# Reading the moving operand of the float32r matmuls as two interleaved streams

## The chip, the cores and the metric

The kernel runs on one core of a Trainium2 chip. The time is the device time of one execution in microseconds (us), the median of three runs. The engines are named as in the profile: PE is TensorE (matmuls), PEld its weight loads, DVE is VectorE, ACT is ScalarE, POOL is GpSimd, and SP is the engine that issues most of the DMA transfers.

## What is computed

One decoder layer on a sequence of 1024 tokens with 1024 channels, all float32: a pooling mixer with a residual, then a gated FFN with a short causal convolution and a second residual.

```python
def reference(x, ...):                      # x (1, 1024, 1024)
    h = rms_norm(x, norm_mix_g[0])
    x = x + pool_mixer(h, pool_w[0], pool_b[0], pool_scale[0])
    f = conv_ffn(rms_norm(x, norm_ffn_g[0]), ffn_w_in[0], ffn_conv_w[0], ffn_conv_b[0], ffn_w_out[0])
    return x + f

def conv_ffn(x, w_in, conv_w, conv_b, w_out):
    h = causal_depthwise_conv(x @ w_in, conv_w, conv_b)   # w_in (1024, 5632), conv over 3 tokens
    val, gate = jnp.split(h, 2, axis=-1)
    return (jax.nn.silu(gate) * val) @ w_out              # w_out (2816, 1024)
```

Nearly all the work is in the two matrix products of the FFN, x @ w_in and the last one.

## The kernel before

**Mixer.** For each of 8 blocks of 128 tokens, plain float32 matmuls form the window sums (psd, L191) and the pooled projection (psy, L274). The residual goes to x1_dram (L281), and the normed block n2 is turned by PE (`ffn_operand`, L303): eight transposes against an identity matrix (pst, L307) give a bank of 128 channels by 128 tokens for each of eight groups of channels. From there ACT and DVE write the operands of the first product.

**First product.** Both products are done with a seven-product block scheme (steps P1 to P7) in place of eight. Its operands are sums and differences of quarters of the two matrices. The token side of the first product stands in tiles B11, B21, T1, T2, T3, B22 and T4 (each 128 partitions, 4 groups of channels, 512 tokens). Each number is stored as two float32r parts, the rounded value and the rest (`split_n`, L323), and each product of two numbers is made from three of the four part products. `product` (L381) runs 12 matmuls into one bank: weights as stationary operand (128x128), 512 tokens as moving operand. There are 22 x 7 such calls, 1848 matmuls. Banks X, Y and Z are read by ACT and DVE (`step`), go through the convolution along the tokens (`conv`), the gate, and are stored in g_dram (L446).

**Second product.** Blocks of g_dram (stationary) and w_out (moving, 512 output channels) are loaded, summed and split by `prep_out` and `split` (L77). The loop over `oevents` runs 4 x 3 matmuls for each event (L744) into four banks, 924 in all, each bank taking eleven events of a step or of two. `z_add` (L660) adds the banks to the residual tiles z by DVE, and the last addition of each tile is followed by its store to `out`. The last bank is done in two halves, the second of them in a bank of its own named rest (L732), so that the first half's add and store run beside the second half's matmuls.

**Order.** The order on each engine is that of the recorded program. Steps P1 to P7 follow a fixed list (`events`), operands are prepared five events ahead (LOOK), in the second product two (OLOOK), with at most about four DVE operations for each event. Columns of all moving operands are read in the order in which they lie.

Of the kernel before, what the change touches and what calls it, by code (L numbers as in the profile page):

```python
# [7 lines left out]
F32 = mybir.dt.float32  # L8
F32R = mybir.dt.float32r
BF16 = mybir.dt.bfloat16  # L10
AF = mybir.ActivationFunctionType
ALU = mybir.AluOpType
PSUM = bass.MemoryType.PSUM

P = 128
# [3 lines left out]
NS = S // P  # L19
NK = D // P  # L20
# [25 lines left out]
NH = 512  # L46
HALVES = [slice(0, NH), slice(NH, D)]
NP2 = NF // 2


@with_exitstack
def trunk_kernel(ctx: ExitStack, tc: tile.TileContext, x, consts, par, rows, pool_w, w_in, w_out, out):
    nc = tc.nc
# [69 lines left out]
    for g, w in enumerate(WINDOWS):  # L123

        m = band[:, g, :]
# [26 lines left out]
    fac = cst[:, FAC:E0].rearrange("p (c t) -> p c t", t=HALO)  # L152
    band_e = cst[:, E0:ID].bitcast(BF16).rearrange("p (g s) -> p g s", s=P)
    ident = cst[:, ID:]
# [79 lines left out]
    def gain_rows():  # L234
        ps = bank2("ps_gain")
        for k in range(NK):
            gain = par_sb[:, GF + k : GF + k + 1].to_broadcast([P, P])
            marks["gain_pe"] = nc.tensor.matmul(ps[:, k * P : (k + 1) * P], gain, ident, start=True, stop=True).ins
        gain_b = pp.tile([P, D], F32, tag="gain_b", name="gain_b")
        marks["gain"] = nc.scalar.activation(gain_b, ps, AF.Copy, scale=FOLD).ins  # L240
        return gain_b
# [61 lines left out]
    def ffn_operand(j):  # L303
        n2 = n2s.pop(j)
        ps = bank2(f"pst{j}")
        for c in range(NK):
            nc.tensor.transpose(ps[:, c * P : (c + 1) * P], n2[:, c * P : (c + 1) * P], ident)  # L307
        cols = slice(j * P, (j + 1) * P)
        ps3 = ps.rearrange("p (c s) -> p c s", c=NK)
        lo, hi = slice(0, 4), slice(4, 8)  # L310
        if j < NS // 2:
            split_n(nops["B11"], ps3[:, lo, :], cols)
            split_n(nops["B21"], ps3[:, hi, :], cols)
            nc.scalar.activation(n2f[:, :, cols], ps3, AF.Copy)
            return
        cols0 = slice(cols.start - NH, cols.stop - NH)
        b11, b12, b21, b22 = n2f[:, lo, cols0], ps3[:, lo, :], n2f[:, hi, cols0], n2f[:, hi, cols]
        nc.scalar.activation(b22, ps3[:, hi, :], AF.Copy)
        sub(b11, b11, b12)
        split_n(nops["T1"], b11, cols0)  # L320
        sub(n2f[:, lo, cols], b22, b12)

    def split_n(t, src, cols=slice(None), ks=slice(None)):  # L323
        h = t[:, 0, ks, cols]
        nc.scalar.activation(h, src, AF.Copy)
        nc.vector.tensor_tensor(t[:, 1, ks, cols], src, h.bitcast(F32), ALU.subtract)  # L326


    order = [j + k * NP2 for j in range(NP2) for k in range(2)]
# [6 lines left out]
    def sub(out, a, b):  # L336
        nc.vector.tensor_tensor(out, a, b, ALU.subtract)  # L337

    def add(out, a, b):
        nc.vector.tensor_tensor(out, a, b, ALU.add)  # L340
# [40 lines left out]
    def product(bank, a, b, opens):  # L381
        m = 0
        for k in range(4):
            ks = slice(k * P, (k + 1) * P)
            for i, l in ((0, 0), (0, 1), (1, 0)):
                nc.tensor.matmul(bank, a[:, i, ks], b[:, l, k, :], start=opens and m == 0, stop=m == 11, skip_group_check=not opens)  # L386
                m += 1

    STEPS = {
# [270 lines left out]
    def z_add(name, set_, rows_, cols, last, rest=None):  # L660
        banks_ = [obanks[set_, i] for i in range(4)]

        def go(i):
            parts = [(slice(0, NH), banks_[i])]
            if rest is not None and i == 3:
                parts = [(slice(0, NH // 2), banks_[i][:, : NH // 2]), (slice(NH // 2, NH), rest[:, : NH // 2])]
            for c, bank in parts:
                z = zs[name, i][:, c]
                add(z, bank, z)
                if last:  # L670
                    r = rows_ * NH + i * P
                    nc.sync.dma_start(out[r : r + P, s_half[cols]][:, c], z)

        chores.extend((go, (i,)) for i in range(4))

# [13 lines left out]
    for k in range(-SLOOK, len(oevents)):  # L689
        p, f = oevents[k + SLOOK] if k + SLOOK < len(oevents) else (None, 0)  # L690
        for _ in range({"P1": 2, "P2": 1, "P5": 1}.get(p, 0)):
            asked[todo[0]] = k + SLOOK
            load_block(*todo.pop(0))
        for name in {"P2": ("A12", "B21"), "P3": ("A12",), "P4": ("B21",)}.get(p, ()):
            load_stream(name, f)
        if k < -OLOOK:
            continue

        with tc.issue_after(lasts[-1]) if lasts else nullcontext():
            room = 4  # L700
            if k + OLOOK < len(oevents):
                e = oevents[k + OLOOK]
                for name in NEEDS.get(e[0], ()):
                    if (name, e[1]) in ahead:
                        do_sum(name, e[1])
                        ahead.remove((name, e[1]))
                        room -= 1
                oops[e] = prep_out(*e)
                room -= 2 + (e[0] in ("P3", "P4"))
            if k < 0:  # L710
                continue
            p, f = oevents[k]
            if chores and f:
                do, args = chores.pop(0)
                for i in args:
                    do(i)
                room -= 1
            while room > 0 and ahead and k >= earliest(*ahead[0]):
                do_sum(*ahead.pop(0))
                room -= 1  # L720
        set_, opens = chains[p]
        if f == 0 and opens:
            for i in range(4):
                tag = ("XXYY" if set_ == "X" else "YZZZ")[i]
                pool = ps_x if tag == "X" else ps_yz
                obanks[set_, i] = pool.tile([P, NH], F32, tag=tag, name=f"o{p}{i}")

        if k >= len(oevents) - TAIL:
            if f < NP2 - 1:
                continue  # L730

            rest = ps_yz.tile([P, NH], F32, tag="Z", name="rest")  # L732
            second = slice(NH // 2, NH)
            add(zs["z21", 3][:, second], obanks[set_, 3][:, second], zs["z21", 3][:, second])
            steps = [(i, g, slice(0, NH), obanks[set_, i]) for i in range(3) for g in range(NP2 - TAIL, NP2)]
            steps += [(3, g, c, t[:, : NH // 2]) for c, t in ((slice(0, NH // 2), obanks[set_, 3]), (second, rest)) for g in range(NP2 - TAIL, NP2)]
        else:
            steps = [(i, f, slice(0, NH), obanks[set_, i]) for i in range(4)]
        for i, g, c, bank in steps:
            a, b = oops[p, g]  # L740
            alone = opens and (p, i) != ("P4", 3)
            for m, (u, v) in enumerate(((0, 0), (0, 1), (1, 0))):
                first = g == (NP2 - TAIL if c.start else 0) and m == 0
                nc.tensor.matmul(  # L744
                    bank, a[:, u, i * P : (i + 1) * P], b[:, v, c],
                    start=opens and first, stop=g == NP2 - 1 and m == 2, skip_group_check=not alone,
                )
        if f == NP2 - 1:
            if p == "P1":
                for i in range(4):  # L750
                    zs["q1", i] = z_tile("q1", i)
                    nc.scalar.activation(zs["q1", i], obanks["X", i], AF.Copy)
                z_start("z11", 0, 0)
            elif p == "P2":
                z_add("z11", "Y", 0, 0, True)
                z_start("z22", 1, 1)
            elif p == "P5":
                z_add("z22", "X", 1, 1, False)
                z_start("z12", 0, 1)
            elif p == "P6":  # L760
                z_add("z12", "Y", 0, 1, False)
            elif p == "P3":
                z_add("z12", "X", 0, 1, True)
                z_start("z21", 1, 0)
            elif p == "P7":
                z_add("z22", "Y", 1, 1, True)
                z_add("z21", "Y", 1, 0, False)
            else:
                z_add("z21", "X", 1, 0, True, rest)
                while chores:  # L770
                    do, args = chores.pop(0)
                    for i in args:
                        do(i)


def constants():
# [11 lines left out]
    def packed(blocks):  # L788
        bits = np.concatenate(blocks, axis=1).astype(np.float32).view(np.uint32)
        assert not (bits & 0xFFFF).any()  # L790
        return np.ascontiguousarray((bits >> 16).astype(np.uint16)).view(np.float32)

    blocks = [packed(first)] + fac + [packed(edge), np.eye(P)]
    return np.concatenate([b.astype(np.float32) for b in blocks], axis=1)


# [32 lines left out]
```

## Time and profile before

| | |
|---|---|
| median of 3 runs | 700.12 us (699.56 to 700.15) |
| the profiled execution | 699.62 us, span 697.7 us |
| HBM traffic | 85.49 MB by DMA, mean 123 GB/s |
| granted TensorE clock | 1.0 in the whole span |

The page gives the busy time of each engine, the busy share in 40 slices of the span, and groups of instructions:

```profile
PE   9999999999999999999999999999999999999998
DVE  4798999999888888888898888876887988999985
DMA  8873113222221211222222221329989700122131
L79 ACT ACTIVATE oBP<-blk 128x512 fp32r<-128x512 f32 x53 | 33.5, 633 | 49.0 <-PE oP L744 32.2
L80 DVE TENSOR_TENSOR oBP<-blk,oBP 128x512 fp32r<-128x512 f32 x53 | 36.6, 691 | 13.3 <-ACT oBP L79 13.3
```

A digit is the busy share of a slice of 17.4 us in tenths, 9 for 90% or more. A group row reads: line, engine, operation, tile written and tiles read, partitions by elements, count; then busy time in us, mean ns of one; then the idle time of the engine just before them and what ended most of it. The length of a matmul in a row holds the time in which it overlaps the next, so the distance from one to the next is shorter than the row's mean. The mixer ends at about 75 us, the first product at 485 us, the second at 694.5 us.

### The profile page before, as it was taken

What the parts mean: (1) busy time and instruction counts of PE and PEld (TensorE: products, weight loads), DVE (VectorE), ACT (ScalarE), POOL (GpSimd) and SP (SyncE); (2) the same over time, 40 slices, a digit from 0 to 9 for tenths busy, and PEclk for the clock granted to TensorE, in tenths of its full rate; (3) what the DMA queues carried; (4) which work ended last, traced back from release to release, by engine and by line L of the source; (5) the groups of instructions that cost most, each with busy time, mean ns of one, the idle gap of its engine ahead of it and who ended that gap; (6) DMA issues with size and microseconds to landing.
All of it is one profiled execution on the core that took longest, in us unless ns stands there. A gap on an engine that the chain in (4) does not pass through costs nothing.

```text
span 697.7 us, 8537 instructions
## 1 busy us (share of the span) xinstructions
PE 692.2 (99%) x3164; PEld 575.5 (82%) x3164; DVE 596.4 (85%) x881; ACT 344.0 (49%) x517; POOL 13.2 (2%) x33
## 2 busy tenths in 40 slices
PE   9999999999999999999999999999999999999998
PEld 7898778888888888888888888888888888888886
DVE  4798999999888888888898888876887988999985
ACT  6787645544444445444454444445454344444431
POOL 3020000000000000000000000000000000000000
PEclk9999999999999999999999999999999999999999
DMA  8873113222221211222222221329989700122131
GB/s 275 296 189 116 62 60 111 102 90 92 91 82 70 88 48 76 92 92 90 91 90 92 89 80 73 99 91 348 326 298 341 273 20 0 61 90 90 63 106 62
DMA packets 32706, 85.49 MB, mean 123 GB/s; under 512 B 3708, under 2 KB 5400, under 8 KB 29848
## 3 DMA queue, kind: packets, MB, share of 16 engines
q1 hardware_dynamic: 31472, 82.83, 33.8%
q0 software_dynamic: 1184, 2.11, 1.8%
q8 instruction: 25, 0.41, 0.2%
q14 instruction: 17, 0.14, 0.1%
q10 hardware_dynamic: 8, 0.00, 0.0%
HBM read 62.89 MB, written 19.92 MB: 119 GB/s over the span
## 4 chain that ended last, share of the span: by engine, by line
PE 92%; DVE 4%; DMA 1%; ACT 1%; issue 1%; SPq 0%; DVEq 0%; ACTq 0%
PE oP L744 30%; PE Y L386 24%; PE Z L386 16%; PE X L386 16%; PE psy L274 3%; PE psd L191 1%; DVE T L326 1%; DMA x<-in_x_dram 1%; PE pst L307 1%; PE psy L277 0%; DVE n2f L337 0%; DVE n2f L562 0%; DVE n2f L555 0%; ACT junk_a L168 0%; PE ps_edges L191 0%
## 5 line engine op out<-in xcount | busy, mean ns | idle before, releaser
L744 PE MATMUL oP<-oBP,oAP 128*128 128x512 f32 (+1 forms) x924 | 208.8, 388 | 0.0
L744 PEld LDWEIGHTS oP<-oBP,oAP 128*128 128x128 f32 x924 | 172.9, 188 | 36.0 <-DVE oBP L80 0.3
L386 PE MATMUL Z<-T,S1s 128*128 128x512 f32 x264 | 64.1, 390 | 0.3 <-DVE T L326 0.2
L386 PE MATMUL X<-B,A11s 128*128 128x512 f32 x264 | 64.2, 390 | 0.0
L386 PE MATMUL Y<-T,S2s 128*128 128x512 f32 x264 | 63.7, 389 | 0.2 <-ACT S2s L79 0.2
L386 PE MATMUL X<-B,A12s 128*128 128x512 f32 x264 | 63.5, 389 | 0.0
L386 PE MATMUL Y<-T,A22s 128*128 128x512 f32 x264 | 63.4, 389 | 0.0
L386 PE MATMUL Y<-T,S3s 128*128 128x512 f32 x264 | 63.4, 389 | 0.0
L386 PE MATMUL Z<-B,S4s 128*128 128x512 f32 x264 | 63.3, 389 | 0.0
L386 PEld LDWEIGHTS Z<-T,S1s 128*128 128x128 f32 x264 | 49.4, 188 | 11.5 <-DVE T L326 0.7
L386 PEld LDWEIGHTS Y<-T,S2s 128*128 128x128 f32 x264 | 49.5, 188 | 10.8 <-ACT S2s L79 0.6
L386 PEld LDWEIGHTS Y<-T,A22s 128*128 128x128 f32 x264 | 49.5, 188 | 10.4
L386 PEld LDWEIGHTS Z<-B,S4s 128*128 128x128 f32 x264 | 49.6, 188 | 10.3
L386 PEld LDWEIGHTS Y<-T,S3s 128*128 128x128 f32 x264 | 49.5, 188 | 10.3
L386 PEld LDWEIGHTS X<-B,A11s 128*128 128x128 f32 x264 | 49.3, 188 | 10.5 <-DVE A11s L80 0.4
L386 PEld LDWEIGHTS X<-B,A12s 128*128 128x128 f32 x264 | 49.5, 188 | 10.2
L79 ACT ACTIVATE oBP<-blk 128x512 fp32r<-128x512 f32 x53 | 33.5, 633 | 49.0 <-PE oP L744 32.2
L80 DVE TENSOR_TENSOR oBP<-blk,oBP 128x512 fp32r<-128x512 f32 x53 | 36.6, 691 | 13.3 <-ACT oBP L79 13.3
L444 ACT ACTIVATE gate<-gate 128x1024 f32<-128x1024 f32 x22 | 23.3, 1061 | 41.9 <-DVE gate L435 41.9
L79 ACT ACTIVATE oAP<-blk 128x512 fp32r<-128x512 f32 x55 | 34.1, 621 | 19.2 <-DVE blk L337 15.9
L340 DVE TENSOR_TENSOR win<-win 128x512 f32<-128x512 f32 x60 | 41.1, 687 | 1.1
L80 DVE TENSOR_TENSOR oAP<-blk,oAP 128x512 fp32r<-128x512 f32 x55 | 37.7, 685 | 2.6 <-ACT oAP L79 2.6
(132 smaller groups left out, 937.8 us busy)
## 6 DMA issues: line engine op xcount, KB each, us to landing
win<-in_w_in_dram SPq DMA_DIRECT2D x22, 1024.0 KB, 4.8
g_dram<-val SPq DMA_DIRECT2D x22, 512.0 KB, 2.6
blk<-g_dram SPq DMA_DIRECT2D x33, 256.0 KB, 5.2
blk<-in_w_out_dram SPq DMA_DIRECT2D x31, 256.0 KB, 5.9
A12s<-g_dram SPq DMA_DIRECT2D x22, 256.0 KB, 5.1
B21s<-in_w_out_dram SPq DMA_DIRECT2D x22, 256.0 KB, 2.8
x_dram<-x SPq DMA_DIRECT2D x8, 512.0 KB, 2.7
z<-x_dram SPq DMA_DIRECT2D x16, 256.0 KB, 5.3
```

The lines of the kernel that those rows point to most:

```text
L79: nc.scalar.activation(t[:, 0, :], src, AF.Copy)
L80: m = nc.vector.tensor_tensor(t[:, 1, :], src, t[:, 0, :].bitcast(F32), ALU.subtract)
L191: m = nc.tensor.matmul(ps[:, c * P : (c + 1) * P], src[:, c * P : (c + 1) * P], weights[:, c // 2, :], start=True, stop=True)
L274: nc.tensor.matmul(o, dh[:, c, :], wps[:, c, :], start=c % 4 == 0, stop=False, skip_group_check=True)
L307: nc.tensor.transpose(ps[:, c * P : (c + 1) * P], n2[:, c * P : (c + 1) * P], ident)
L326: nc.vector.tensor_tensor(t[:, 1, ks, cols], src, h.bitcast(F32), ALU.subtract)
L340: nc.vector.tensor_tensor(out, a, b, ALU.add)
L386: nc.tensor.matmul(bank, a[:, i, ks], b[:, l, k, :], start=opens and m == 0, stop=m == 11, skip_group_check=not opens)
L444: nc.scalar.activation(gate, gate, AF.Silu)
L744: nc.tensor.matmul(bank, a[:, u, i * P : (i + 1) * P], b[:, v, c], start=opens and first, stop=g == NP2 - 1 and m == 2, skip_group_check=n ...
```

## The change

The 512 columns of the moving operand are read in the order 0, 256, 1, 257 and so on to 255, 511: two streams of 256 in turns (`woven`). To leave the results as they were, the columns are stored or read elsewhere in the order that goes with it.

- First product: the tokens in the operand tiles are stored with even tokens in the first 256 places and odd ones in the second. The identity matrix that turns the tokens has its columns in the order even, odd (`turn`), so a turned block of 128 tokens comes as 64 even and 64 odd ones, and ACT and DVE write two runs of 64 in place of one of 128. Read in turns, the columns come in the order of the tokens, so the banks and what follows are unchanged.
- Second product: w_out lies as before. Read in turns, its channels 0, 256, 1, 257 and so on come to the bank in that order, and who reads the bank (`z_add` on DVE, the copy q1 on ACT) takes the places 0, 2, 4 ... for channels 0 to 255 and 1, 3, 5 ... for the rest (`apart`). The halves of the last bank are now the channels 0 to 127 with 256 to 383, and the rest.

```diff
+def woven(t):
+    return t.rearrange("p (a b) -> p b a", a=2)
+def apart(bank):
+    return bank.rearrange("p (b a) -> p a b", a=2)
+def halved(t, n=2):
+    return t.rearrange("p (a b) -> p a b", a=n)
...
-            marks["gain_pe"] = nc.tensor.matmul(ps[:, k * P : (k + 1) * P], gain, ident, start=True, stop=True).ins
+            marks["gain_pe"] = nc.tensor.matmul(ps[:, k * P : (k + 1) * P], gain, woven(ident), start=True, stop=True).ins
...
-        ps3 = ps.rearrange("p (c s) -> p c s", c=NK)
+        ps3 = ps.rearrange("p (c a s) -> p c a s", c=NK, a=2)
...
+        half, q = divmod(j, NS // 2)
+        cols = slice(q * P // 2, (q + 1) * P // 2)
+        here, first = (n2f[:, :, h * NH : (h + 1) * NH].rearrange("p c (a s) -> p c a s", a=2)[:, :, :, cols] for h in (half, 0))
...
-                nc.tensor.matmul(bank, a[:, i, ks], b[:, l, k, :], start=opens and m == 0, stop=m == 11, skip_group_check=not opens)
+                nc.tensor.matmul(bank, a[:, i, ks], woven(b[:, l, k, :]), start=opens and m == 0, stop=m == 11, skip_group_check=not opens)
...
-                z = zs[name, i][:, c]
-                add(z, bank, z)
+                z = halved(zs[name, i])[:, :, c]
+                add(z, apart(bank), z)
...
-                    bank, a[:, u, i * P : (i + 1) * P], b[:, v, c],
+                    bank, a[:, u, i * P : (i + 1) * P], woven(b[:, v, :])[:, c.start // 2 : c.stop // 2, :],
...
-                    nc.scalar.activation(zs["q1", i], obanks["X", i], AF.Copy)
+                    nc.scalar.activation(halved(zs["q1", i]), apart(obanks["X", i]), AF.Copy)
...
-    blocks = [packed(first)] + fac + [packed(edge), np.eye(P)]
+    turn = np.eye(P).reshape(P, P // 2, 2).transpose(0, 2, 1).reshape(P, P)
+    blocks = [packed(first)] + fac + [packed(edge), turn]
```

No instruction is added, removed or moved on any engine; PE's and POOL's rows differ in their line numbers alone. What differs on the others is the shape of some accesses. ACT, where it takes turned tokens from the banks pst into the tiles B and n2f, before:

```order
L325 ACTIVATE B_155<-pst_411 128x4x128
L168 ACTIVATE junk_b_401,st_b_402<-x_146 128x1024
L325 ACTIVATE B_157<-pst_411 128x4x128
L169 ACTIVATE st_b_402<-st_b_402,eps_t 128x1
L168 ACTIVATE junk_a_431,st_a_432<-x_231 128x1024
L314 ACTIVATE n2f<-pst_411 128x8x128
```

and the same place now:

```order
L338 ACTIVATE B_155<-pst_411 128x8x64
L180 ACTIVATE junk_b_401,st_b_402<-x_146 128x1024
L338 ACTIVATE B_157<-pst_411 128x8x64
L181 ACTIVATE st_b_402<-st_b_402,eps_t 128x1
L180 ACTIVATE junk_a_431,st_a_432<-x_231 128x1024
L328 ACTIVATE n2f<-pst_411 128x8x2x64
```

The order stands, and each group of 128 tokens is written as two runs of 64. DVE at the end of the program, with the last additions to the output tiles z, before:

```order
L80 TENSOR_TENSOR oBP_10_5498<-B21s_5452,oBP_10_5498 128x512
L340 TENSOR_TENSOR z_0_5184<-oP_5322,z_0_5184 128x512
L340 TENSOR_TENSOR z_1_5186<-oP_5323,z_1_5186 128x512
L340 TENSOR_TENSOR z_2_5207<-oP_5324,z_2_5207 128x512
L340 TENSOR_TENSOR z_3_5209<-oP_5325,z_3_5209 128x256
L340 TENSOR_TENSOR z_3_5209<-rest,z_3_5209 128x256
```

and now:

```order
L92 TENSOR_TENSOR oBP_10_5498<-B21s_5452,oBP_10_5498 128x512
L353 TENSOR_TENSOR z_0_5184<-oP_5322,z_0_5184 128x512
L353 TENSOR_TENSOR z_1_5186<-oP_5323,z_1_5186 128x512
L353 TENSOR_TENSOR z_2_5207<-oP_5324,z_2_5207 128x512
L353 TENSOR_TENSOR z_3_5209<-oP_5325,z_3_5209 128x2x128
L353 TENSOR_TENSOR z_3_5209<-rest,z_3_5209 128x2x128
```

The additions are as many and as large; the halves of the last tile are two runs of 128 channels each.

More of the change, by code (lines that the diff above doesn't have):

```diff
@@ L307, in ffn_operand, with split_n @@
             nc.tensor.transpose(ps[:, c * P : (c + 1) * P], n2[:, c * P : (c + 1) * P], ident)
-        cols = slice(j * P, (j + 1) * P)
-        ps3 = ps.rearrange("p (c s) -> p c s", c=NK)
+        ps3 = ps.rearrange("p (c a s) -> p c a s", c=NK, a=2)
         lo, hi = slice(0, 4), slice(4, 8)
[L311 to L314, printed above, removed]
+        half, q = divmod(j, NS // 2)
+        cols = slice(q * P // 2, (q + 1) * P // 2)
+        here, first = (n2f[:, :, h * NH : (h + 1) * NH].rearrange("p c (a s) -> p c a s", a=2)[:, :, :, cols] for h in (half, 0))
+        if half == 0:
+            split_n(nops["B11"], ps3[:, lo], cols)
+            split_n(nops["B21"], ps3[:, hi], cols)
+            nc.scalar.activation(here, ps3, AF.Copy)
             return
-        cols0 = slice(cols.start - NH, cols.stop - NH)
-        b11, b12, b21, b22 = n2f[:, lo, cols0], ps3[:, lo, :], n2f[:, hi, cols0], n2f[:, hi, cols]
-        nc.scalar.activation(b22, ps3[:, hi, :], AF.Copy)
+        b11, b12, b22 = first[:, lo], ps3[:, lo], here[:, hi]
+        nc.scalar.activation(b22, ps3[:, hi], AF.Copy)
         sub(b11, b11, b12)
[L320 to L324, printed above, removed]
+        split_n(nops["T1"], b11, cols)
+        sub(here[:, lo], b22, b12)
+    def split_n(t, src, cols=None, ks=slice(None)):
+        h, l = (t[:, i, ks] if cols is None else t[:, i].rearrange("p k (a s) -> p k a s", a=2)[:, :, :, cols] for i in range(2))
         nc.scalar.activation(h, src, AF.Copy)
-        nc.vector.tensor_tensor(t[:, 1, ks, cols], src, h.bitcast(F32), ALU.subtract)
+        nc.vector.tensor_tensor(l, src, h.bitcast(F32), ALU.subtract)
     order = [j + k * NP2 for j in range(NP2) for k in range(2)]
@@ L663, in go @@
         def go(i):
-            parts = [(slice(0, NH), banks_[i])]
+            parts = [(slice(0, NH // 2), banks_[i])]
             if rest is not None and i == 3:
-                parts = [(slice(0, NH // 2), banks_[i][:, : NH // 2]), (slice(NH // 2, NH), rest[:, : NH // 2])]
+                parts = [(slice(0, NH // 4), banks_[i][:, : NH // 2]), (slice(NH // 4, NH // 2), rest[:, : NH // 2])]
             for c, bank in parts:
-                z = zs[name, i][:, c]
-                add(z, bank, z)
+                z = halved(zs[name, i])[:, :, c]
+                add(z, apart(bank), z)
                 if last:
                     r = rows_ * NH + i * P
-                    nc.sync.dma_start(out[r : r + P, s_half[cols]][:, c], z)
+                    nc.sync.dma_start(halved(out[r : r + P, s_half[cols]])[:, :, c], z)
         chores.extend((go, (i,)) for i in range(4))
@@ L733, in trunk_kernel @@
             second = slice(NH // 2, NH)
-            add(zs["z21", 3][:, second], obanks[set_, 3][:, second], zs["z21", 3][:, second])
+            z = halved(zs["z21", 3])[:, :, NH // 4 :]
+            add(z, apart(obanks[set_, 3][:, second]), z)
             steps = [(i, g, slice(0, NH), obanks[set_, i]) for i in range(3) for g in range(NP2 - TAIL, NP2)]
```

## The prediction

> **What bounds the kernel now.** I read the page from the top: the busy times, then the chain of work that ended last, then the groups on that chain. The profiled execution took 699.62 us for a span of 697.7 us; the median of the three timed runs is 700.12 us, 0.07% more, so a sum made against 699.6 us stands for the median too.
>
> ```profile
> span 697.7 us, 8537 instructions
> PE 692.2 (99%) x3164; PEld 575.5 (82%) x3164; DVE 596.4 (85%) x881; ACT 344.0 (49%) x517; POOL 13.2 (2%) x33
> PE oP L744 30%; PE Y L386 24%; PE Z L386 16%; PE X L386 16%; PE psy L274 3%; PE psd L191 1%; DVE T L326 1%; DMA x<-in_x_dram 1%; PE pst L307 1%; PE psy L277 0%; DVE n2f L337 0%; DVE n2f L562 0%; DVE n2f L555 0%; ACT junk_a L168 0%; PE ps_edges L191 0%
> L744 PE MATMUL oP<-oBP,oAP 128*128 128x512 f32 (+1 forms) x924 | 208.8, 388 | 0.0
> L386 PE MATMUL Z<-T,S1s 128*128 128x512 f32 x264 | 64.1, 390 | 0.3 <-DVE T L326 0.2
> ```
>
> TensorE (PE) is busy 99% of the span, and the two lines that the change touches, L386 and L744, hold 86% of the chain. Seven groups like the last row (7 x 264 = 1848) and the 924 of L744 make 2772 matmuls. They wait for nothing (0.3 us and 0.0 us of idle time). So the time is 2772 times the distance from one matmul to the next, plus the stage before. That distance is not the 388 ns of a row, since matmuls overlap; the chain in order of time gives it, with start, length and count:
>
> ```profile
> 484.75 208.67 PE oP L744 x924
> 346.04 2.72 PE Z L386 x12
> 46.09 3.46 PE psy L274 x16
> 50.01 0.87 PE pst L307 x8
> 44.30 1.79 PE psd L191 x16
> ```
>
> In both products a matmul of 512 columns takes 2.72/12 = 226.7 ns (208.67/924 = 225.8 ns, with some short ones in it). [...] The plain float32 matmuls ahead of them are slower per column: psy, 256 columns, 3.46/16 = 216.3 ns; pst, 128 columns, 0.87/8 = 108.8 ns; psd, 128 columns, 1.79/16 = 111.9 ns. The merged timeline shows the shorter form of the float32r matmul, and the groups of PE and of weight loads by shape give the rest:
>
> ```profile
> 693.26 1.24 PE L744 MATMUL rest<-oBP,oAP 128*128 128x256 f32 x9
> L744 PE MATMUL rest<-oBP,oAP 128*128 128x256 f32 x9 | 1.2, 283 | 0.0
> L386 PEld LDWEIGHTS Y<-T,S2s 128*128 128x128 f32 x264 | 49.5, 188 | 10.8 <-ACT S2s L79 0.6
> L274 PEld LDWEIGHTS psy<-wps,dh 128*128 128x128 f32 x128 | 23.9, 190 | 3.1
> ```
>
> A float32r matmul of 256 columns takes (1.24 - 0.283)/8 = 119.6 ns. From 512 to 256 columns the difference is 107.1 ns, 0.418 ns a column, which leaves 2 x 119.6 - 226.7 = 12.5 ns per matmul that do not depend on the columns. The same for plain float32, 256 against 128 columns: 0.84 ns a column and 2 x 108.8 - 216.3 = 1.3 ns fixed with pst, 0.815 ns a column and 2 x 111.9 - 216.3 = 7.5 ns with psd. The weight load is the same (188 and 190 ns, 128x128). So **a matmul whose columns arrive every 0.42 ns pays 5 to 11 ns of fixed cost that one with columns every 0.84 ns does not pay.**
>
> **The change, part by part.** No instruction is added, removed or moved on any engine; only the patterns differ.
>
> (1) The moving operand of all 2772 matmuls. Column 0 is followed by column 256, then 1, 257, and so on: two places 1 KB apart, each advancing one column per 0.84 ns, which is the pace of the plain float32 products. No row of this trace shows such a read. Its cost is bounded by the rows above: at best the fixed 12.5 ns go; at worst a column costs 0.84 ns instead of 0.418 ns. The row nearest in pace for each stream is that of the plain products, with 1.3 to 7.5 ns fixed. I take 2.5 ns, nearer to pst, because a pst is one instruction per call, as a float32r matmul is. That is 10 ns less per matmul, with -12.5 and +203 to +212 ns as the far ends.
>
> What of the 10 ns is on the path is read by stages, with DVE (VectorE) beside PE:
>
> ```profile
> core 0: us, PE busy (x) PEld busy (x) DVE busy (x) ACT busy (x) POOL busy (x), PEclk, DMA share, GB/s
> 64.00:102.00 38.00, 37.46 (x174) 29.91 (x173) 37.81 (x52) 21.79 (x32) 0.00 (x0) 1.00 0.20 70
> 102.00:160.00 58.00, 58.00 (x257) 48.04 (x256) 56.31 (x75) 30.84 (x43) 0.00 (x0) 1.00 0.26 91
> 160.00:484.00 324.00, 324.00 (x1431) 268.38 (x1430) 272.80 (x351) 152.69 (x205) 0.00 (x0) 1.00 0.27 95
> 484.75:693.42 208.67, 208.67 (x927) 172.79 (x926) 181.77 (x286) 92.29 (x154) 0.00 (x0) 1.00 0.43 149
> ```
>
> Up to 102 us DVE is busy 37.81 of 38.00 us: nothing is gained there, since PE would only wait for DVE. From 102 to 160 us, 257 x 10 ns = 2.6 us would be saved, but DVE has 56.31 us to do in 58.00 us, so 1.7 us at most: what is late next is DVE, which preps the next operands. From 160 to 484 us: 324/0.2267 = 1429 matmuls x 10 ns = 14.3 us; DVE at 272.80 us fits into 309.7 us. Second product: 924 x 10 ns = 9.2 us; DVE's 181.77 us fits into 199.5 us. DMA moves 149 GB/s there at a share of 0.43. Together -25.2 us.
>
> [...]
>
> (2) Reads of banks with step 2: each output bank is now read as even and odd places.
>
> ```profile
> L340 DVE TENSOR_TENSOR z<-oP,z 128x512 f32<-128x512 f32 x27 | 18.4, 683 | 3.3 <-PE oP L744 3.3
> L340 DVE TENSOR_TENSOR z<-z,q 128x512 f32<-128x512 f32 x16 | 10.9, 683 | 0.0
> L752 ACT ACTIVATE q<-oP 128x512 f32<-128x512 f32 x4 | 2.2, 592 | 0.1
> L340 DVE TENSOR_TENSOR z<-rest,z 128x256 f32<-128x256 f32 x1 | 0.4, 425 | 0.7 <-PE rest L744 0.7
> ```
>
> The last of these rows is in the tail, see (4). Some 28 adds of 683 ns (27 and halves) read a bank. An add from a bank costs what one from SBUF costs (683 ns both), so the place of the operand does not set the pace, and step 2 is likely free: I take 0, with +683 ns each, 19 us of DVE, as the other end (below nothing is excluded, as the same elements are read). Cover: DVE has 208.67 - 181.77 = 26.9 us free in the second product, 17.7 us if PE is faster. At the dear end DVE would have 200.9 us to do against 199.5 us, and the stage would keep 1 us less of its gain, or up to 9 us where several adds fall together. The four q copies (592 ns, ACT busy 92 of 209 us) are hidden at either end.
>
> (3) Tokens written in runs of 64 instead of 128 (L325, L318, L314, L337 on ACT and DVE).
>
> ```profile
> L325 ACT ACTIVATE B<-pst 128x512 fp32r<-128x512 f32 x8 | 4.7, 592 | 2.1 <-PE pst L307 2.0
> L326 DVE TENSOR_TENSOR B<-pst,B 128x512 fp32r<-128x512 f32 x8 | 5.5, 688 | 0.5 <-ACT B L325 0.3
> L258 DVE TENSOR_TENSOR psd<-psd,edges 128x128 f32<-128x128 f32 x6 | 1.8, 294 | 1.7 <-ACT edges L203 1.1 <-PE psd L191 0.6
> ```
>
> Today's runs of 128 (688 ns on DVE) take within 5 ns what whole rows of 512 take (683 ns). The last row reads and writes 8 runs of 16: 294 ns, where 683 and 425 ns for 512 and 256 elements in a row lead to 296 ns for 128. So runs even of 16 cost nothing: 0, and at most these 5 ns on each of 40 pieces, 0.2 us.
>
> (4) The tail. After the last matmul come one add and one store.
>
> ```profile
> out_dram<-z SPq DMA_DIRECT2D x15, 256.0 KB, 2.4
> out_dram<-z SPq DMA_DIRECT2D x2, 128.0 KB, 1.9
> ```
>
> That add (425 ns) may double, so 0 to 0.43 us; the store of 128 KB goes out in runs of 512 B instead of 1 KB, and I bound it by that of twice the size: 0 to 2.4 - 1.9 = 0.5 us. I take +0.3 us together.
>
> Sum: 699.6 - 25.2 + 0.3 = **674.7 us**. With the fixed part gone wholly (12.5 ns: 17.9 + 11.6 + 1.7 = 31.2 us) 668.7 us; with only 5 ns gone (7.1 + 4.6 + 1.3 = 13.0 us) 686.9 us.
>
> **The rivals.** (A) The fixed part is not the moving operand's: it comes with each float32r matmul, whatever it reads, and the distance stays 226.7 ns. For it: the cost is the same in two products with different tiles, and does not grow with the columns. Against it: equal weight loads beside slower columns hardly show it. Then the time is 699.6 + 0.3 = 699.9 us; or, if (2) is dear and half of its 19 us comes late for PE, 709 us.
>
> (B) **Slower: each column is fetched on its own.** [...] In the new order no two successive columns are neighbours. If the read then delivers a column per 0.84 ns, as the plain products' columns come, a matmul takes 512 x 0.815 to 0.84 + 12.5 = 430 to 443 ns, 203 to 216 ns more; 2772 times that is 563 to 599 us, and the time about 1280 us. It decides from 226.7/512 = 0.443 ns a column: above that the change loses even with no fixed cost left. For it: the float32r products are the only ones that need a column per 0.42 ns, so they have the least to spare. [...]
>
> [...]
>
> **How the numbers follow.** Forecast, the fixed part mostly goes: 0.44. (A) 0.36: 0.24 within 0.2% (1.4 us, about what a measurement of this kernel can tell from no change), 0.10 slower through dear step-2 adds, 0.02 faster. (B) 0.20. So faster 0.46, within 0.2% 0.24, slower 0.30. The range leaves (B) out, at 0.20, and takes in the rest: from 665 us (the whole fixed part and a little of the DVE stage) to 711 us ((A) with dear adds and the dear tail). The forecast's own range is 665 to 690 us.
>
> **What would show it.** In the chain after, the pieces of 12 matmuls of L386 should be 2.60 us instead of 2.72 us, and the 924 of the second product 199.5 us. At 2.72 us (A) holds; at 5.1 us or more (B). The z adds should stay at 683 ns; DVE idle time before PE's matmuls of T and S2s should appear up to 160 us. The forecast is wrong if the distance between matmuls does not fall below 224 ns.

## The result, and the profile after

| | before | after |
|---|---|---|
| median | 699.91 us (4 runs, 699.56 to 700.15) | 672.80 us (4 runs, 672.28 to 674.00) |
| ratio | | 0.9615, 95% interval 0.9599 to 0.9632 |
| profiled execution, its span | 699.62 us, 697.7 us | 672.94 us, 671.1 us |

The kernel became 27.1 us faster, 3.85% (3.68 to 4.01%). The prediction said 674.7 us. The page of the changed kernel, in the order in which the one of before was read (busy times, chain, groups; L758 was L744, L399 was L386):

```profile
span 671.1 us, 8537 instructions
PE 663.3 (99%) x3164; PEld 578.5 (86%) x3164; DVE 591.6 (88%) x881; ACT 338.3 (50%) x517; POOL 13.1 (2%) x33
PE 75%; DVE 19%; ACT 2%; DMA 2%; issue 1%; SPq 0%; ACTq 0%; DVEq 0%
L758 PE MATMUL oP<-oBP,oAP 128*128 128x512 f32 (+1 forms) x924 | 198.9, 378 | 0.1
L399 PE MATMUL Z<-T,S1s 128*128 128x512 f32 x264 | 61.2, 380 | 0.6 <-DVE T L339 0.3
```

PE is still busy 99% of the span and still waits for almost nothing, but DVE now holds 19% of the chain (4% before): the two engines have come close. The share overstates it. From 574 to 661 us the chain runs through ACT and DVE, which prepare operands there, yet PE idles only 0.11 us in the whole second product (last row of the stages below). The chain in order of time shows the distance between matmuls and where the time went, with start, length and count of each piece:

```profile
58.07 2.59 PE X L399 x12
...
159.76 2.59 PE X L399 x12
...
467.97 106.20 PE oP L758 x492
...
666.84 1.02 PE rest L758 x9
```

A matmul of 512 columns now takes 2.59/12 = 215.8 ns instead of 226.7 ns, 10.9 ns less. The same pieces of the chain of before, for the stages:

```profile
57.47 2.77 PE X L386 x12
...
161.08 2.72 PE X L386 x12
...
484.75 208.67 PE oP L744 x924
693.42 1.09 PE rest L744 x9
```

| stage, from piece to piece | before | after | saved |
|---|---|---|---|
| up to the first product | 57.47 | 58.07 | -0.6 |
| to the product at 161 us | 103.61 | 101.69 | 1.9 |
| to the second product | 323.67 | 308.21 | 15.5 |
| second product to its last half bank | 208.67 | 198.87 | 9.8 |
| the rest | 4.28 | 4.26 | 0.0 |
| span | 697.7 | 671.1 | 26.6 |

The first row is the mixer, where the change touches only the 16 matmuls `ps_gain` that read the identity matrix; they cost 0.4 us more (shown under the first experiment). The other 0.2 us is no more than the scatter of the start: with the order alone, which leaves the mixer as it was, the first product starts at 57.74 us. In the stage up to 160 us PE now waits for DVE, and in the second product hardly at all:

```profile
core 0: us, PE busy (x) PEld busy (x) DVE busy (x) ACT busy (x) POOL busy (x), PEclk, DMA share, GB/s
64.66:102.00 37.34, 35.86 (x172) 29.59 (x171) 37.34 (x52) 21.51 (x32) 0.00 (x0) 1.00 0.19 71
102.00:160.00 58.00, 57.42 (x264) 49.35 (x263) 56.42 (x76) 31.04 (x44) 0.00 (x0) 1.00 0.25 91
160.00:467.97 307.97, 307.97 (x1428) 269.68 (x1428) 270.99 (x352) 149.33 (x204) 0.00 (x0) 1.00 0.28 100
467.97:666.84 198.87, 198.76 (x927) 173.86 (x926) 179.94 (x286) 89.98 (x154) 0.00 (x0) 1.00 0.45 158
```

From 64.66 to 102 us DVE is busy in every moment and PE in 35.86 of 37.34 us. Up to 160 us PE idles 1.48 + 0.58 = 2.1 us; before, it idled 0.5 us from 64 to 160 us. The groups of the adds and copies that read a bank with step 2:

```profile
L353 DVE TENSOR_TENSOR z<-oP,z 128x512 f32<-128x512 f32 x27 | 18.5, 684 | 3.1 <-PE oP L758 3.1
L353 DVE TENSOR_TENSOR z<-rest,z 128x256 f32<-128x256 f32 x1 | 0.4, 425 | 0.6 <-PE rest L758 0.6
L766 ACT ACTIVATE q<-oP 128x512 f32<-128x512 f32 x4 | 2.1, 594 | 0.0
```

They took 683, 425 and 592 ns before: step 2 costs at most 2 ns each here.

### The profile page after: what moved, and what is told of

It reads as the page before. It is cut to its first block, busy times and chain, and to the rows that moved or that the text cites. A ratio compares the mean times of both kernels' runs of the same rounds, so it can differ in the third digit from the quotient of the medians.

```text
span 671.1 us, 8537 instructions
## 1 busy us (share of the span) xinstructions
PE 663.3 (99%) x3164; PEld 578.5 (86%) x3164; DVE 591.6 (88%) x881; ACT 338.3 (50%) x517; POOL 13.1 (2%) x33
## 4 chain that ended last, share of the span: by engine, by line
PE 75%; DVE 19%; ACT 2%; DMA 2%; issue 1%; SPq 0%; ACTq 0%; DVEq 0%
PE Y L399 22%; PE oP L758 17%; PE X L399 14%; PE Z L399 14%; PE psy L286 4%; DVE oAP L92 3%; DVE oBP L92 3%; PE psd L203 2%; ACT oAP L91 2%; DVE T L339 1%; DVE z L353 1%; DVE blk L350 1%; DVE A12s L350 1%; DVE B21s L350 1%; DMA win<-in_w_in_dram 1%
## 5 line engine op out<-in xcount | busy, mean ns | idle before, releaser
L758 PE MATMUL oP<-oBP,oAP 128*128 128x512 f32 (+1 forms) x924 | 198.9, 378 | 0.1
L758 PEld LDWEIGHTS oP<-oBP,oAP 128*128 128x128 f32 x924 | 174.0, 189 | 25.1 <-DVE oBP L92 0.5
L399 PE MATMUL Z<-T,S1s 128*128 128x512 f32 x264 | 61.2, 380 | 0.6 <-DVE T L339 0.3
L399 PE MATMUL X<-B,A11s 128*128 128x512 f32 x264 | 61.3, 380 | 0.2 <-DVE A11s L92 0.2
L399 PE MATMUL Y<-T,S3s 128*128 128x512 f32 x264 | 60.8, 380 | 0.6 <-DVE q L428 0.6
L399 PE MATMUL Y<-T,S2s 128*128 128x512 f32 x264 | 60.8, 379 | 0.5 <-ACT S2s L91 0.5
L399 PE MATMUL Y<-T,A22s 128*128 128x512 f32 x264 | 60.8, 380 | 0.2 <-DVE hb L436 0.2
L399 PE MATMUL X<-B,A12s 128*128 128x512 f32 x264 | 60.7, 379 | 0.0
L399 PE MATMUL Z<-B,S4s 128*128 128x512 f32 x264 | 60.4, 379 | 0.0
L399 PEld LDWEIGHTS Z<-T,S1s 128*128 128x128 f32 x264 | 49.7, 189 | 8.6 <-DVE T L339 0.7
L399 PEld LDWEIGHTS Y<-T,S3s 128*128 128x128 f32 x264 | 49.7, 189 | 8.3 <-DVE q L428 1.4
L399 PEld LDWEIGHTS Y<-T,S2s 128*128 128x128 f32 x264 | 49.8, 189 | 7.9 <-ACT S2s L91 0.9
L399 PEld LDWEIGHTS Y<-T,A22s 128*128 128x128 f32 x264 | 49.7, 189 | 8.0 <-DVE hb L436 1.0
L399 PEld LDWEIGHTS X<-B,A11s 128*128 128x128 f32 x264 | 49.7, 189 | 7.6 <-DVE A11s L92 0.6
L399 PEld LDWEIGHTS Z<-B,S4s 128*128 128x128 f32 x264 | 49.9, 189 | 7.1
L399 PEld LDWEIGHTS X<-B,A12s 128*128 128x128 f32 x264 | 49.8, 189 | 7.0
```

The costliest lines, as they stand in the source:

```text
L399: nc.tensor.matmul(bank, a[:, i, ks], woven(b[:, l, k, :]), start=opens and m == 0, stop=m == 11, skip_group_check=not opens)
L758: nc.tensor.matmul(bank, a[:, u, i * P : (i + 1) * P], woven(b[:, v, :])[:, c.start // 2 : c.stop // 2, :], start=opens and first, stop=g ...
```

## The experiments

The prediction's reason was the pace of the moving operand's read. What in the order of the columns sets that pace was open. Theories that were weighed, in the letters of the expectations:

- **S**, two places read in turns, each advancing by neighbours;
- **L**, successive columns must not lie in one group of four neighbours;
- **F**, the mere form of the pattern;
- **C**, a fetch for each column;
- **B**, two banks of the memory that must lie far apart (not the prediction's rival (B));
- **P**, the prediction's half pace for each place;
- **D**, columns fetched in twos;
- **W**, the weight load's reads hold up the moving read;
- **T**, formed on the way: columns in even and in odd positions are read by two lanes.

Each kernel is the one of before with the order of the columns changed at the two matmul calls alone, without the storage that goes with it, so the results are permuted. Most change the moving columns, two change the weights' columns instead, and one changes both; the eighteen matmuls of 256 columns at the end stay contiguous. Each ran once, beside one run of the kernel before on the same chip (699.21, 700.29 and 700.45 us for the three groups of four).

```diff
+def turned(t):
+    return t.rearrange(..., ...)
...
-                nc.tensor.matmul(bank, a[:, i, ks], b[:, l, k, :], start=opens and m == 0, stop=m == 11, skip_group_check=not opens)
+                nc.tensor.matmul(bank, a[:, i, ks], turned(b[:, l, k, :]), start=opens and m == 0, stop=m == 11, skip_group_check=not opens)
...
-                    bank, a[:, u, i * P : (i + 1) * P], b[:, v, c],
+                    bank, a[:, u, i * P : (i + 1) * P], turned(b[:, v, :]) if c == slice(0, NH) else b[:, v, c],
```

What follows gives the inside of `turned` for each.

**The order alone.**

```diff
+    return t.rearrange("p (a b) -> p b a", a=2)
```

> The kernel before with the two-stream order at the two matmul calls alone (256-column tail pieces stay contiguous); storage and readers of banks stay as before, so tokens and channels come out permuted. If the whole gain is the read order of the moving operand: 2.59 us per 12 matmuls and about 672.8 us, within 0.5 us of the full change. If the other parts (runs of 64, bank reads with step 2, tail) cost something, this run is faster than the full change by that, up to 2 us.

672.45 us against 672.80 us for the whole change, with 2.59 us per 12 matmuls. The whole gain is the read order; runs of 64, bank reads with step 2 and the new halves at the end cost nothing that can be told from the scatter of 672.28 to 674.00 us. One other cost shows in the chains, first of this run, then of the whole change:

```profile
9.00 1.79 PE ps_gain L242 x16
```

```profile
9.30 2.18 PE ps_gain L250 x16
```

These are plain float32 matmuls of 128 columns. This run reads the identity matrix as it lies, the whole change reads it as two streams of 64. A matmul takes 1.79/16 = 111.9 ns here and 2.18/16 = 136.3 ns there: the order that helps the float32r matmuls slows these. No run tells why.

**One stream with step 2.**

```diff
+    return t.rearrange("p (b a) -> p a b", a=2)
```

> Moving columns in the order 0, 2, 4 ... 510, then 1, 3 ... 511: one stream with step 2; results permuted. Theory S (two places far apart must be read in turns): 226.7 ns per matmul, 700 us. Theory L (successive columns must not lie in the same group of four neighbours): two successive ones still share a group, so 226.7 ns or something between, 686 to 700 us. Theory F (any pattern of two dimensions takes another path): 215.8 ns, 673 us. Theory C (a column per place costs a fetch): 700 us or more.

1319.23 us. **One stream with step 4:**

```diff
+    return t.rearrange("p (b a) -> p a b", a=4)
```

> Moving columns in the order 0, 4, 8 ... 508, then 1, 5 ...: one stream with step 4, no two successive columns within a group of four neighbours; results permuted. Theory S (two far places in turns): 226.7 ns per matmul, 700 us. Theory L (successive columns in different groups of four): 215.8 ns, 673 us. Theory F (form of the pattern): 673 us. If it were slower than 226.7 ns, the read rate of single places would be the limit and turns between two held places the reason why the change does not suffer.

1345.98 us. In the chains, first of step 2, then of step 4:

```profile
303.73 5.41 PE Z L390 x12
```

```profile
302.09 5.54 PE Y L390 x12
```

That is 5.41/12 = 450.8 ns and 5.54/12 = 461.7 ns per matmul, about twice 226.7 ns. L falls (step 4 never stays in a group of four), and F falls (two dimensions, and slower). S as written had expected 700 us, so it did not hold either: it had no price for columns of one stream that are not neighbours, and these two orders paid 224 and 235 ns more. C had said 700 us or more, and is not contradicted by these two. A price near that of rival (B) of the prediction, a column per 0.84 ns, is thus paid (450.8/512 = 0.88 ns and 461.7/512 = 0.90 ns), but in other orders than that of the change.

**Blocks of 128 of the two halves in turns.**

```diff
+    return t.rearrange("p (a c b) -> p c a b", a=2, b=128)
```

> Moving columns in blocks of 128: 0 to 127, 256 to 383, 128 to 255, 384 to 511; results permuted. A pattern of three dimensions whose columns are neighbours all but three times. Theory F (form of the pattern): 215.8 ns per matmul, 673 us. Theories S and L (order of successive columns): 226.7 ns, 700 us.

701.03 us and 2.72 us per 12 matmuls: a pattern of three dimensions with neighbours in a row takes the time of the contiguous one (2.72 us). F is out.

**Two places 4 columns apart, then 32 columns apart.**

```diff
+    return t.rearrange("p (c a b) -> p c b a", a=2, b=4)
...
+    return t.rearrange("p (c a b) -> p c b a", a=2, b=32)
```

> Moving columns in turns from two places only 4 columns (16 bytes) apart: 0, 4, 1, 5, 2, 6, 3, 7, then 8, 12 ...; results permuted. Theory S, as amended by the runs with step 2 and 4 (a column after a column from the same place is cheap only if it lies beside that place's last one, whatever the distance of the two places): each place advances by neighbours, so 215.8 ns per matmul, 673 us. Theory B (two successive columns come from two banks of the memory, far apart, and conflict if they are near): 451 to 461 ns as with steps 2 and 4, about 1320 to 1350 us.

> As the run with 4 columns between the two places, with 32 columns (128 bytes): 0, 32, 1, 33 ... 31, 63, then 64 ...; results permuted. Theory S: 215.8 ns per matmul, 673 us. Theory B: depends on where the banks part: 673 us if 128 bytes are far enough, about 1320 us if not. Together with the run of 4 columns it says whether distance matters at all.

672.14 and 673.40 us, both with 2.59 us per 12 matmuls. The two places may lie 16 bytes, 128 bytes or, as in the change, 1 KB apart: the distance does not matter among these three. B is out, and so is C, since no two successive columns are neighbours here.

**Pairs from the two halves in turns.**

```diff
+    return t.rearrange("p (a c b) -> p c a b", a=2, b=2)
```

> Moving columns in pairs from the two places 1 KB apart: 0, 1, 256, 257, 2, 3, ...; results permuted. If the gain comes from successive columns being asked of two places in turns: between 215.8 and 226.7 ns, since every other step is to the neighbour; a pair has the same two places and pace on average, so theory P of the prediction (each place advances at half pace) says 215.8 ns and 673 us. Theory D (the memory is read two columns at a time, and the two of one read must come from two places to leave room for the weight load) says 226.7 ns and 700 us, or about twice as slow if the turn between pairs itself costs.

979.31 us; the chain has

```profile
301.25 3.94 PE Y L390 x12
```

so 328.3 ns per matmul. None of the numbers of the expectation, D's included: P is wrong, although each place advances by neighbours and at half pace here too. What differs from the two-stream order is the position of a column: 0, 1, 256, 257 against 0, 256, 1, 257. Looked at by every second position, the fast orders read 0, 1, 2, 3 ... there, the contiguous order 0, 2, 4, 6, step 2 reads 0, 4, 8, and pairs read 0, 256, 2, 258. From this came theory T, in which each of the two lanes reads by groups of four neighbours.

**Weights with step 4.**

```diff
-                nc.tensor.matmul(bank, a[:, i, ks], b[:, l, k, :], start=opens and m == 0, stop=m == 11, skip_group_check=not opens)
+                nc.tensor.matmul(bank, a[:, i, k :: 4], b[:, l, k, :], start=opens and m == 0, stop=m == 11, skip_group_check=not opens)
...
-                    bank, a[:, u, i * P : (i + 1) * P], b[:, v, c],
+                    bank, a[:, u, i :: 4], b[:, v, c],
```

> Moving columns contiguous as before; the stationary operand of both products is read with step 4, so its 128 columns are spread over four times the memory; output rows are mixed up. Theory W (the fixed 10.8 ns are the weight load's reads, which hold up the moving read): up to four times as many reads, 226.7 + 3 x 10.8 = 259 ns per matmul, 788 us. If the fixed cost is the moving operand's own (its start or end): 226.7 ns, 700 us.

724.85 us and 2.82/12 = 235.0 ns per matmul. This one does not tell: the weight load itself became the limit. Its group by shape, and the matmuls of 256 columns at the end in the chain:

```profile
L744 PEld LDWEIGHTS oP<-oBP,oAP 128*128 128x128 f32 x924 | 217.3, 310 | 0.1
```

```profile
717.63 2.12 PE rest L744 x9
```

The load takes 310 ns (188 before) and PEld has 0.1 us of idle time left. The nine matmuls of 256 columns, 1.09 us in the chain before, now take 2.12 us, that is 2.12/9 = 235.6 ns for each, about as long as one of 512. W's 259 ns and 788 us were not reached. The next runs therefore used step 2 for the weights, and tested T.

**Two places 2 columns apart.**

```diff
+    return t.rearrange("p (c a b) -> p c b a", a=2, b=2)
```

> Moving columns 0, 2, 1, 3, then 4, 6, 5, 7 and so on: the two places are 2 columns apart; results permuted. Theory T (the columns in even and in odd positions of the order are read by two lanes, each reading a group of four neighbours (16 bytes) at a time; the contiguous order uses each group twice in a lane, the two-stream order four times, steps 2 and 4 once): each lane reads 0, 1, 4, 5 ..., two columns of a group, as in the contiguous order, so 226.7 ns per matmul and 700 us. Theory S (each place advances by neighbours, whatever the distance): 215.8 ns, 673 us.

699.73 us, 2.72 us per 12 matmuls: T's number, not S's. Two places in turns gain nothing when they lie 2 columns apart; T puts that down to each lane's meeting only two columns of a group in a row, as in the contiguous order.

**Fours from the two halves in turns.**

```diff
+    return t.rearrange("p (a c b) -> p c a b", a=2, b=4)
```

> Moving columns 0 to 3, 256 to 259, 4 to 7, 260 to 263 and so on; results permuted. Theory T: each lane reads two columns of a group and then goes to a group elsewhere, the same number of groups as in the contiguous order, so 226.7 ns per matmul and 700 us. If a change of place costs by itself, as half of the 328 ns of the order in pairs suggests, more: about 250 to 280 ns, 760 to 850 us. Theory S: 215.8 ns.

762.73 us, and in the chain

```profile
301.71 3.00 PE Z L390 x12
```

250.0 ns, the lower end of what the expectation gave for a change of place that costs by itself, and not T's number. By T a lane reads as many columns of a group in a row as in the contiguous order, yet a matmul takes 23 ns more; there are 127 changes of place in it, so 0.18 ns for each. In the pairs it would be 101.6 ns for 255 changes, 0.40 ns for each. So T without a cost of changing place is not enough, and one fixed cost for each change does not fit both orders.

**Weights with step 2, moving columns contiguous; then with the moving columns in two streams.** `evens(k)` gives the columns k % 2, k % 2 + 2 ... of the k // 2-th block of 256.

```diff
+def evens(k):
+    return slice(k // 2 * 256 + k % 2, k // 2 * 256 + 256, 2)
...
-                nc.tensor.matmul(bank, a[:, i, ks], b[:, l, k, :], start=opens and m == 0, stop=m == 11, skip_group_check=not opens)
+                nc.tensor.matmul(bank, a[:, i, evens(k)], b[:, l, k, :], start=opens and m == 0, stop=m == 11, skip_group_check=not opens)
...
-                    bank, a[:, u, i * P : (i + 1) * P], b[:, v, c],
+                    bank, a[:, u, evens(i)], b[:, v, c],
```

> Moving columns contiguous as before; the 128 columns of the stationary operand are read with step 2, so they lie in twice as many groups of four; output rows are mixed up. Theory W (each group that the weight load reads holds up a contiguous moving read, which has no room to spare): twice the fixed cost above the 2.5 ns, 226.7 + 10.8 = 237.5 ns per matmul, 730 us, if the weight load itself (188 ns now, 310 ns at step 4) stays short enough to be hidden. If the fixed cost is the moving operand's own: 226.7 ns, 700 us.

> Stationary operand with step 2 as in the run beside it, and the moving columns in two streams of 256 in turns; rows and columns of the results are mixed up. Theory W with T (the two-stream order leaves room for the weight load's reads): 215.8 to 217 ns per matmul, 673 us, however many groups the weight load reads, as long as it is hidden. If the weight load with step 2 is too long to be hidden, both runs show the same distance, above 216 ns, and W stays open.

717.36 and 672.87 us. The chain and the weight loads by shape, of the contiguous one:

```profile
300.56 2.80 PE X L390 x12
...
L748 PEld LDWEIGHTS oP<-oBP,oAP 128*128 128x128 f32 x924 | 177.8, 193 | 37.1 <-DVE oBP L84 0.2
```

and of the one with two streams:

```profile
301.95 2.59 PE Y L394 x12
...
L752 PEld LDWEIGHTS oP<-oBP,oAP 128*128 128x128 f32 x924 | 180.6, 196 | 18.5 <-DVE oBP L88 0.5
```

The loads are about as long as before (193 and 196 ns against 188 ns) and have idle time left, so they are hidden. With contiguous columns the distance grows from 226.7 to 2.80/12 = 233.3 ns when the weights are spread over twice the memory; with two streams it stays at 215.8 ns. So weights at step 2 make a matmul of 512 contiguous columns longer, and one of 512 columns in two streams not. The size was off: 6.7 ns more, not 10.8 ns. And it is not so much for each load: the nine contiguous matmuls of 256 columns at the end of the same run, with the same weights at step 2, take 1.09 us in the chain, as they do before. That the weight load's reads hold up the moving read, and that the 10.9 ns of the change are this and nothing else, is therefore argued (W), not shown.

## Why the prediction was right

**The cost that goes.** The prediction took 10 ns off each matmul of 512 columns; 10.9 ns went (215.8 ns measured, 216.7 ns forecast). The run with the order alone shows that the gain is that of the read order. That it is a fixed cost per matmul that goes is only half borne out. The last matmuls of the changed kernel have 256 columns, read in two streams as well:

```profile
666.67 1.17 PE L758 MATMUL rest<-oBP,oAP 128*128 128x256 f32 x9
```

With 0.275 us as the mean length of one they are (1.17 - 0.275)/8 = 111.9 ns apart, against 119.6 ns before. By the prediction's own working that leaves 2 x 111.9 - 215.8 = 8.0 ns fixed, where 2.5 ns was forecast, and 0.406 ns a column, where 0.418 ns was kept. So about half of the 10.9 ns came off the columns, which the sum took as unchanged, and the fixed part shrank by only some 5 ns, the size with which the prediction had reckoned 686.9 us. That the columns gave the rest was not foreseen. (The nine matmuls are few, and whether their weight loads set their pace is not shown.)

**So the size was in part luck.** No run shows the 2.5 ns: they were the author's estimate between the 1.3 and 7.5 ns of the plain float32 rows, made because of the half pace of each stream, and the same working gives 8.0 ns after the change. And "two places, each at half pace" is not what decides: pairs and fours have it too and are slower than before, and two places 2 columns apart have it and gain nothing. The plain float32 matmuls themselves got slower when they were read in two streams (111.9 to 136.3 ns). What the runs point to is how many neighbours meet in every second position. The contiguous order and the nine others, sorted by it:

| order | every second position | ns per matmul |
|---|---|---|
| two streams, 4, 32 or 256 columns apart | 0, 1, 2, 3 | 215.8 |
| contiguous; blocks of 128; two streams 2 apart | 0, 2, 4, 6; 0, 1, 4, 5 | 226.7 |
| fours | 0, 2, 256, 258 | 250.0 |
| pairs | 0, 256, 2, 258 | 328.3 |
| step 2 | 0, 4, 8 | 450.8 |
| step 4 | 0, 8, 16 | 461.7 |

Read so, four columns of a group of four in a row are best (215.8 ns), two give the pace of before (226.7 ns), one about halves it (450.8 and 461.7 ns). Two rows do not fit: fours have two like the contiguous order and take 23 ns more, and pairs have one like step 2 and take some 120 ns less. That the read has two lanes is a reading of this table, not something a profile shows; how a change of place is paid in fours and pairs stays open, and with it why the change gains what it gains.

**Stages.** Forecast and measured: to 160 us 1.7 and 1.9 us (PE's idle time grew from 0.5 to 2.1 us there, behind DVE, as its busy share said), rest of the first product 14.3 and 15.5 us, second 9.2 and 9.8 us, tail +0.3 and 0.0 us. The 0.6 us that the span lost ahead of the first float32r product was not forecast; 0.4 us of it are the 16 `ps_gain` matmuls, which the prediction's count of 2772 left out.

**Step 2 on the banks, runs of 64:** taken as free, and free (684 against 683 ns for an add, 687 against 688 ns for the pieces in runs of 64, and the run with the order alone).

**Rival (A)**, that the fixed cost comes whatever is read, is refuted by the run with the order alone. **Rival (B)**, each column fetched on its own, was priced at 430 to 443 ns (that is 203 to 216 ns more; the +212 ns that part (1) names as the far end does not follow from its rows). Steps 2 and 4 come near that price (451 and 462 ns), so such orders exist; that the change escapes it because each lane stays in its group is theory T, not shown.

**DVE as the next limit** was read from its busy times, and is seen up to 160 us. In the second product it only ties with PE: it holds much of the chain there, and PE idles 0.11 us.

## What to carry to other kernels

Where back-to-back matmuls take more than their columns, compare matmuls of two lengths and two rates in the same trace; that gives an idea of what an edit can win, but do the same working again afterwards, since here the split into a cost per column and a cost per matmul did not hold. For float32r matmuls with a weight load each, reading the moving columns as two interleaved streams took 10.9 of 226.7 ns here. Places 4, 32 and 256 columns apart served alike (215.8 ns each), so among these the distance can be chosen for the convenience of storage; 2 columns apart gained nothing (226.7 ns), and step 2 alone about doubled the time of a matmul (450.8 ns). Leave plain float32 matmuls out of it until they are measured: the 16 here got slower (111.9 to 136.3 ns). Try the read order alone first, with permuted results: it gave all but 0.4 us of the answer without any storage rearranged.

## What was not expected of the hardware

- A float32r matmul with its moving operand at step 2 takes 450.8 ns per 512 columns instead of 226.7 ns, and step 4 hardly more (461.7 ns).
- The same columns, read in pairs from two halves, take 328.3 ns, in single columns from two halves 215.8 ns.
- A weight load with step 2 takes 193 ns against 188 ns; with step 4, 310 ns, and then sets the pace of the matmuls (235.0 ns, with 0.1 us of idle time left to the 924 loads).
- Weights at step 2 slow a contiguous float32r moving read of 512 columns (226.7 to 233.3 ns), but not one of 256 columns (1.09 us in the chain for nine with either) and not the two-stream read (215.8 ns with either).
- A plain float32 matmul of 128 columns takes 136.3 ns with its moving columns read as two streams, 111.9 ns with them in order.
